# Tying TensorE's narrow products of two attention steps and of the sample rows into one visit

## The chip, the cores and the metric

The kernel runs on one core of a Trainium2 chip. The metric is the device time of one execution in microseconds (us), as the median over several runs. A profile of one further execution stands beside it. The engines are TensorE (PE, and PEld for its weight loads), VectorE (DVE), ScalarE (ACT), GpSimd (POOL) and SyncE (SP, which issues DMAs).

## The reference

One inference step of one decoder layer, in float32: 2048 prompt tokens and 8 sample tokens (one for each of 8 sequences with 2048 past tokens), model width 1024.

```python
u = x @ w_in                       # 1024 -> 7 x 512: q_a k_a v_a | q_r k_r v_r | g_r
# A: 8 heads x 64, three dilated windows (128,1), (512,4), (2048,16) with a bias on the logits;
#    the three branches are mixed in proportion to their softmax denominators
# B: 4 retention heads of 128, chunks of 128 with a decayed state, rotary q/k, per-head norm, gate
mix = concat(A, B) @ w_out
x1  = LN1(alpha * x + mix)
y   = LN2(alpha * x1 + relu(x1 @ w_up)**2 @ w_down)
```

For a sample token the attention reads 3 x 128 gathered rows of a key/value cache and its own key and value, and retention updates one 128 x 128 state for each head. Outputs are y for prompt and sample, the new key/value rows, and the retention states.

## The kernel before

Everything is kept transposed, features on the 128 partitions. The prompt is cut into four blocks j of 512 tokens. The phases follow each other: input projection of blocks 0 and 1, output projection of block 0, input projection of blocks 2 and 3, output projections of blocks 1, 2 and 3, then the feed-forward part in three passes. A float32 product with a projection or feed-forward weight is done as three products of rounded operands (high x high, high x low, low x high; `gps`, `vps` for the projections).

An input projection has 28 tiles m of 128 output features, in an order by head pair t or retention head: queries and keys of retention, the two v tiles (tiles 2 and 5, done together with x as the weights in `gemm_flip`), the gate, queries and keys of attention. Other work is woven into these tiles. Each tile calls `mid` once, which advances the attention by one step, and `end` once, which pops jobs of queues.

- **Attention steps.** `make_steps` gives a head pair in block j 4 steps (blocks 0 and 1) or 6 (blocks 2 and 3). `attn_advance` is a pipeline over them: products with v of the step before last (`attn_pv`, L687, into `o`), transposes of the last one (`attn_tr`, L656, into `ptps`), logits of a new one (`attn_qk`, L630 and L631, into `sps`). After the logits, VectorE adds the bias table and takes the row's minimum (L644), ScalarE the exponential (L645) into `p`. After the transposes, ScalarE copies those of head x = 0 (L659) and VectorE those of x = 1 (L661) to `ptile`, which has four buffers. Each product with v is 64 columns wide: the two heads of a pair write the two halves of the output's partitions. In the trace each float32 product of this kind stands as two instructions, a transpose as one.
- **Sample rows.** `sample_jobs` makes a list of jobs that `end` pops one at a time, from block 1 on: rotary, logits over gathered keys, a softmax, then for each of 8 sequences `pv(b)`: `f` (gathered values times weights, `spv`, L981) and `g` (a sum over 32-row groups, `spd`, L991, and the loads of the next sequence's values `svg`), and for each of 4 heads x 2 halves `ret(h, bh)`: `f` (state update on VectorE) and `g` (query times state, `sro`, L1026, and the loads of the next state). These products are 32 columns wide, four to a bank side by side (`tile_position`). In block 0, `v_sample` (L562, `vss`) does the sample's v rows in the same way from the raw weight tile, right where `w_split` splits that tile, twice for each t; `ev_v` then adds the four groups (`svn`, L545).
- **Retention.** `ret_stages` gives for each head and block five stages r0 to r4: transposed keys (`rtp`), scores (`rs`, L811) and state increments (`rd`, L817) with the chain of states on VectorE (`rst`, L823), outputs (`ro`, L830 and L831) and norm, transposes back (`ryt`) with the gate, store.

The code gives a program order. A scheduler with a cost model then orders the instructions of each engine: one whose operands are there, by the model, may go ahead of one traced earlier that still waits. Each engine runs its list in order. `keep_in_program_order(ins)` adds an edge for the order only, behind the instruction traced just before it on the same engine; `add_manual_dep` with class Sync adds a real dependency. `end` goes through its queues with this rule, where an entry holds a function and what it takes of two allowances t and s:

```python
t = s = 2
for q in (self.vprep, self.fin, self.rets, self.smpj):
    if q and q[0][1] <= t and q[0][2] <= s:
        f, dt, ds = q.pop(0)
        t, s = t - dt, s - ds
        f()
```

The functions that the diff touches, and their callers:

Of the kernel before, what the change touches and what calls it, by code (L numbers as in the profile page):

```python
# [9 lines left out]
F32 = mybir.dt.float32  # L10
# [50 lines left out]
class Trunk:  # L61
# [105 lines left out]
    def w_split(self, k):  # L167
        if k in self.wraw:
# [4 lines left out]
            if k in self.vsk:  # L173
                self.v_sample(*self.vsk[k], w)
# [157 lines left out]

    def gemm(self, ps, w, x, c0, n, mid=None, ks=None):
# [54 lines left out]
    def gemm_phase(self, nm, evac, mid, end, nxt=None, pre=None, before_next=None, flip=lambda m: 0):  # L388
# [3 lines left out]
        for m in range(nm - 1):  # L392
# [35 lines left out]
    def gemm_flip(self, m, evac, mid, end):  # L428
# [4 lines left out]
        for half in range(2):  # L433
            ps = self.bank(self.pg, "vps")
            for b in range(2):
                if b:
                    mid(m + half)
                    self.w_split(self.wdue)
# [9 lines left out]
    def attn_open(self):  # L448
# [13 lines left out]
        self.steps, self.sa, self.sb = [], None, None  # L462
# [76 lines left out]
    def ev_v(self, t, half, ps):  # L539
        nc, at = self.nc, self.at  # L540
        if half is None:
            v = at.tile([P, 512], F32, tag="p", name=self.nm("svn"), bufs=4)[:NB, :256]
            nc.vector.tensor_copy(v, ps[0:NB])
            for g in range(1, 4):
                nc.vector.tensor_tensor(out=v, in0=ps[32 * g:32 * g + NB], in1=v, op=OP.add)  # L545
            sl = slice(t * P, (t + 1) * P)
# [9 lines left out]
    def v_sample(self, t, half, w):  # L556

        if half == 0:
            self.vsp = self.bank(self.pt, "vss", 256)
        for k in range(4):  # L560
            g = 32 * k
            self.nc.tensor.matmul(self.vsp[g:g + NB], self.xs[:, 4 * half + k, :], w[:, 256 * k:256 * k + 256],  # L562
                                  start=(half == 0), stop=(half == 1), tile_position=(0, g))
        if half:
            self.ev_v(t, None, self.vsp)
# [28 lines left out]
    def attn_qk(self, s):  # L594
# [4 lines left out]
        for x in range(2):  # L599
# [43 lines left out]
            for d2, view, t2, dst, sl in post:  # L643
                nc.vector.tensor_tensor_reduce(d2, view, t2, 1.0, 3e38, OP.add, OP.min, sl[0])  # L644
                nc.scalar.activation(dst, dst, AF.Exp, bias=sl[0], scale=-1.0, accum_out=sl[1])  # L645
# [3 lines left out]
    def attn_tr(self, s):  # L649
        nc = self.nc  # L650
        s["PT"] = []
        tot = sum(w for _, w in s["w"])
        for x in range(2):
            b = self.bank(self.pt, "ptps", tot)
            for k in range(tot // P):
                nc.tensor.transpose(b[:, k * P:(k + 1) * P], s["P"][x][:, k * P:(k + 1) * P], self.ident)  # L656
            d = self.at.tile([P, 512], F32, tag="ptile", name=self.nm("ptile"), bufs=4)
            if x == 0:
                nc.scalar.copy(d[:, :tot], b)  # L659
            else:  # L660
                nc.vector.tensor_copy(d[:, :tot], b)  # L661
            s["PT"].append(d)

    def attn_pv(self, s):
# [6 lines left out]
        for (col, w), u in zip(s["w"], s["units"]):  # L671
            nk = w // P
            for k in range(nk):
                for x in range(2):
# [12 lines left out]
                    nc.tensor.matmul(out, v, s["PT"][x][:, col + k * P:col + (k + 1) * P],  # L687
                                     start=(k == 0), stop=(k == nk - 1))
# [1207 lines left out]
```

## Time and profile before

| what | value |
|---|---|
| median of 3 runs | 2618.89 us (2618.74 to 2621.79) |
| profiled execution, its own time | 2621.11 us |
| span of its profile, first to last instruction | 2619.3 us |
| TensorE products busy | 2571.3 us, 98% |
| TensorE weight loads busy | 2380.0 us, 91% |
| VectorE busy | 1778.6 us, 68% |
| ScalarE busy | 1260.3 us, 48% |
| mean granted TensorE clock | 0.994 |

In the profile's rows an instruction is named by its line, engine, operation, output tile and inputs (`o<-ptile,v`), then the shape (`128*64 128x128`: weights of 128 rows and 64 columns, moving operand of 128 x 128) and a count. Timeline rows give start and duration in us and merge neighbours of one kind; a matmul's duration includes its way through the array, so the time that it holds TensorE is read from start to start.

### The profile page before, as it was taken

To read this page: it belongs to the slowest core of one execution; us is meant where nothing else is said; L and a number is where in the kernel's file an instruction comes from. 1 tells how busy PE (TensorE), PEld (TensorE's weight loads), DVE (VectorE), ACT (ScalarE), POOL (GpSimd) and SP (SyncE) were. 2 spreads that over 40 slices of the span, in tenths; PEclk is the share of its full clock that TensorE was granted. 3 is DMA by queue.
4 is the path that set the end of the run, shared out by engine and by line. 5 is a ranking of instruction groups with operands and counts; after the bars stand their busy time and mean duration, and the time that the engine had idled before them with its cause. 6 is when DMAs were issued, how large, how long until landed. Compare 5 with 4: busy or idle time off the path is not lost.

```text
span 2619.3 us, 44506 instructions
## 1 busy us (share of the span) xinstructions
PE 2571.3 (98%) x16852; PEld 2380.0 (91%) x16852; DVE 1778.6 (68%) x3751; ACT 1260.3 (48%) x2632; POOL 89.2 (3%) x119
## 2 busy tenths in 40 slices
PE   8999999999999999989999999999999999999998
PEld 7999778877788788788999999999999999999998
DVE  5677886655676766679888666578775547755567
ACT  4456445444443555445565433356654336544336
POOL 0000320000110000000000000100000010000000
PEclk9999999999999999999999999999999999999999
DMA  7345764664666344578557332854484295433322
GB/s 257 115 127 181 225 184 145 210 212 141 190 193 202 117 152 148 163 228 280 204 185 261 119 113 101 306 190 153 158 265 133 93 301 197 164 111 102 100 89 76
DMA packets 233099, 451.36 MB, mean 172 GB/s; under 512 B 33665, under 2 KB 122434, under 8 KB 232339
## 3 DMA queue, kind: packets, MB, share of 16 engines
q1 hardware_dynamic: 210532, 403.07, 47.5%
q0 software_dynamic: 12864, 32.20, 3.9%
q10 hardware_dynamic: 9488, 13.24, 1.5%
q8 instruction: 133, 2.18, 0.4%
q14 instruction: 82, 0.67, 0.1%
HBM read 346.30 MB, written 102.12 MB: 171 GB/s over the span
## 4 chain that ended last, share of the span: by engine, by line
PE 51%; DMA 2%; DVE 2%; ACT 1%; issue 0%; SPq 0%; DVEq 0%; ACTq 0%
PE dps L1662 9%; PE dps L1663 9%; PE dps L1664 9%; PE ups L1603 7%; PE ups L1604 7%; PE ups L1605 7%; DMA xr<-hd 1%; PE gps L343 1%; PE gps L344 1%; PE gps L345 1%; DMA fr<-in_w_up 0%; DVE zc L1216 0%; DMA zc<-x1d 0%; DVE zc L1188 0%; DVE wl L356 0%
## 5 line engine op out<-in xcount | busy, mean ns | idle before, releaser
L1662 PE MATMUL dps<-hid,fh 128*128 128x344 f32 (+2 forms) x1544 | 487.9, 318 | 3.0 <-ACT fh L351 2.6
L1663 PE MATMUL dps<-hid,fh 128*128 128x344 f32 (+2 forms) x1544 | 490.3, 318 | 0.0
L1664 PE MATMUL dps<-hid,fl 128*128 128x344 f32 (+2 forms) x1544 | 480.0, 318 | 0.0
L1603 PE MATMUL ups<-fx,fu 128*128 128x344 f32 (+1 forms) x1344 | 429.1, 320 | 1.1 <-DVE rl L1627 0.7
L1604 PE MATMUL ups<-fx,fu 128*128 128x344 f32 (+1 forms) x1344 | 429.8, 320 | 0.0
L1605 PE MATMUL ups<-fx,fu 128*128 128x344 f32 (+1 forms) x1344 | 421.7, 319 | 0.8 <-DVE fu L356 0.6
L343 PE MATMUL gps<-xh,wh 128*128 128x512 f32 (+2 forms) x1120 | 398.7, 360 | 19.7 <-ACT xh L351 12.6
L345 PE MATMUL gps<-xh,wl 128*128 128x512 f32 (+2 forms) x1120 | 396.9, 355 | 0.9 <-DVE wl L356 0.8
L344 PE MATMUL gps<-xl,wh 128*128 128x512 f32 (+2 forms) x1120 | 397.0, 356 | 0.5 <-DVE xl L356 0.5
L351 ACT ACTIVATE fu<-fr 128x512 fp32r<-128x512 f32 x320 | 192.8, 627 | 348.1 <-PE dps L1663 235.0
L1671 DVE TENSOR_TENSOR ya<-dps,ya 128x344 f32<-128x344 f32 (+2 forms) x344 | 170.9, 504 | 194.7 <-PE dps L1664 192.8
L1662 PEld LDWEIGHTS dps<-hid,fh 128*128 128x128 f32 x1544 | 290.2, 188 | 3.5 <-ACT fh L351 2.9
L1663 PEld LDWEIGHTS dps<-hid,fh 128*128 128x128 f32 x1544 | 290.9, 188 | 0.0
L1664 PEld LDWEIGHTS dps<-hid,fl 128*128 128x128 f32 x1544 | 288.2, 188 | 0.2 <-DVE fl L356 0.2
L343 PEld LDWEIGHTS gps<-xh,wh 128*128 128x128 f32 x1120 | 212.7, 191 | 56.8 <-ACT xh L351 14.6
L1603 PEld LDWEIGHTS ups<-fx,fu 128*128 128x128 f32 x1344 | 252.6, 188 | 1.7 <-DVE rl L1627 1.0
L1604 PEld LDWEIGHTS ups<-fx,fu 128*128 128x128 f32 x1344 | 252.6, 188 | 0.0
L1605 PEld LDWEIGHTS ups<-fx,fu 128*128 128x128 f32 x1344 | 251.3, 188 | 1.3 <-DVE fu L356 1.3
L344 PEld LDWEIGHTS gps<-xl,wh 128*128 128x128 f32 x1120 | 213.7, 191 | 34.3 <-issue 5.4
L356 DVE TENSOR_TENSOR fu<-fr,fu 128x512 fp32r<-128x512 f32 x320 | 214.4, 690 | 43.0 <-ACT fu L351 41.1
L345 PEld LDWEIGHTS gps<-xh,wl 128*128 128x128 f32 x1120 | 213.7, 191 | 31.6 <-DVE wl L356 2.4
L356 DVE TENSOR_TENSOR wl<-wr,wh 128x1024 fp32r<-128x1024 f32 (+1 forms) x147 | 177.4, 1209 | 57.9 <-ACT wh L351 57.1
(256 smaller groups left out, 4269.6 us busy)
## 6 DMA issues: line engine op xcount, KB each, us to landing
wr<-in_w_in SPq DMA_DIRECT2D x111, 512.0 KB
fr<-in_w_down SPq DMA_DIRECT2D x96, 512.0 KB
fr<-in_w_up SPq DMA_DIRECT2D x64, 512.0 KB
fr<-wsd SPq DMA_DIRECT2D x64, 512.0 KB
xr<-in_x SPq DMA_DIRECT2D x64, 256.0 KB
wr<-in_w_out SPq DMA_DIRECT2D x32, 512.0 KB
wsd<-fr SPq DMA_DIRECT2D x48, 256.0 KB
t<-modd SPq DMA_DIRECT2D x16, 512.0 KB
```

Source lines behind the costliest of these rows:

```text
L343: mm(ps, wh, xh[:, c0:c0 + n], start=(k == 0), stop=False)
L344: mm(ps, wh, xl[:, c0:c0 + n], start=False, stop=False)
L345: mm(ps, wl, xh[:, c0:c0 + n], start=False, stop=(k == last))
L351: nc.scalar.activation(h, raw, AF.Copy)
L356: (nc.vector if eng_l == "v" else nc.gpsimd).tensor_tensor(out=l, in0=raw, in1=f32(h), op=OP.subtract)
L1603: mm(ps, wh, xh[:, k, :n], start=start and k == 0, stop=False, skip_group_check=not start)
L1604: mm(ps, wh, xl[:, k, :n], start=False, stop=False, skip_group_check=not start)
L1605: mm(ps, wl, xh[:, k, :n], start=False, stop=k == 3, skip_group_check=not start)
L1662: mm(ps, wh, xh, start=(k == 0), stop=False)
L1663: mm(ps, wh, xl, start=False, stop=False)
L1664: mm(ps, wl, xh, start=False, stop=(k == 3))
L1671: nc.vector.tensor_tensor(out=y, in0=ps, in1=y, op=OP.add)
```

## The change

Products with v of two attention steps, and the sample rows' 32-column products, are issued together.

- `attn_advance` keeps up to two transposed steps in `sb` and issues both steps' products with v when there are two (or when no further step is under way). Ahead of them come queued `v_sample` groups, behind them one job of the sample list that is marked "part". Such jobs (`spv`, `spd`, `sro`) are popped there alone; when nothing else is due, one goes at the second advance.
- `mm` issues a product through `pin`: within a visit, every one but the first is kept in program order behind the one before. The first product with v gets a dependency on the four copies of both steps (`cp`). The first transpose of a step gets one on the step's last exponential.
- `v_sample` is queued by `w_split` and issued at the next advance, each half in its own bank; `ev_v` adds half 0 to `svn` and then half 1. A v tile is split ahead of the `mid` call.
- In the sample list, `pm` is prepared one job ahead (`prep`), the next values are loaded in `spv`'s job, the next state in `ret`'s `f`.
- In retention's r1 the state increments and their chain come ahead of the scores, and an empty stage stands between r2 and r3.

```diff
     def w_split(self, k):
             if k in self.vsk:
-                self.v_sample(*self.vsk[k], w)
+                self.vsq.append((*self.vsk[k], w))

+    def pin(self, ins, after=()):
+        if self.visit:
+            self.tc.keep_in_program_order(ins)
+        elif self.visit == 0:
+            self.visit = 1
+        self.gate(ins, after)
+        return ins
+
+    def gate(self, ins, after):
+        for x in after:
+            self.tc.add_manual_dep(ins.ins, x.ins.name, mybir.DependencyInfo(mybir.DependencyClass.Sync,
+                                   mybir.DependencyReason.DATA), reason="visit")
+
+    def mm(self, *a, after=(), **k):
+        return self.pin(self.nc.tensor.matmul(*a, **k), after)

     # gemm_phase, ahead of mid(mm); the same in gemm_flip
+                        if k == len(w) // 2 and self.wdue in self.vsk:
+                            self.w_split(self.wdue)

     def ev_v(self, t, half, ps):
-        if half is None:
-            v = at.tile([P, 512], F32, tag="p", name=self.nm("svn"), bufs=4)[:NB, :256]
-            nc.vector.tensor_copy(v, ps[0:NB])
-            for g in range(1, 4):
+        if half in ("s0", "s1"):
+            if half == "s0":
+                self.svn = at.tile([P, 512], F32, tag="p", name=self.nm("svn"), bufs=4)[:NB, :256]
+                nc.vector.tensor_copy(self.svn, ps[0:NB])
+            v = self.svn
+            for g in range(half == "s0", 4):
                 nc.vector.tensor_tensor(out=v, in0=ps[32 * g:32 * g + NB], in1=v, op=OP.add)
+            if half == "s0":
+                return

     def v_sample(self, t, half, w):
-        if half == 0:
-            self.vsp = self.bank(self.pt, "vss", 256)
+        vsp = self.bank(self.pt, "vss", 256)
         for k in range(4):
             g = 32 * k
-            self.nc.tensor.matmul(self.vsp[g:g + NB], ..., start=(half == 0), stop=(half == 1), tile_position=(0, g))
-        if half:
-            self.ev_v(t, None, self.vsp)
+            self.mm(vsp[g:g + NB], ..., start=True, stop=True, tile_position=(0, g))
+        self.ev_v(t, "s%d" % half, vsp)

     # attn_qk keeps the step's last exponential: s["exp"] = [e]
     def attn_tr(self, s):
-                nc.tensor.transpose(b[:, k * P:(k + 1) * P], s["P"][x][:, k * P:(k + 1) * P], self.ident)
+                i = nc.tensor.transpose(b[:, k * P:(k + 1) * P], s["P"][x][:, k * P:(k + 1) * P], self.ident)
+                self.gate(i, s["exp"] if x == k == 0 else ())
...
+            s["cp"].append((nc.vector.tensor_copy if x else nc.scalar.copy)(d[:, :tot], b))

     # attn_pv(s, after)
-                    nc.tensor.matmul(out, v, s["PT"][x][:, col + k * P:col + (k + 1) * P],
-                                     start=(k == 0), stop=(k == nk - 1))
+                    self.mm(out, v, s["PT"][x][:, col + k * P:col + (k + 1) * P],
+                                     start=(k == 0), stop=(k == nk - 1), after=after)
+                    after = ()

     def attn_advance(self):
-        if self.sb is not None:
-            self.attn_pv(self.sb)
-            self.sb = None
+        part = bool(self.vsq)
+        self.visit = 0
+        for v in self.vsq:
+            self.v_sample(*v)
+        self.vsq = []
+        if len(self.sb) == 2 or (self.sb and self.sa is None):
+            part = True
+            after = [x for s in self.sb for x in s["cp"]]
+            for s in self.sb:
+                self.attn_pv(s, after)
+                after = ()
+            self.sb = []
+        if self.smpj and self.smpj[0][1] == "part":
+            self.late += 1
+            if part or self.late == 2:
+                self.smpj.pop(0)[0]()
+                self.late = 0
+        self.visit = None
         if self.sa is not None:
             self.attn_tr(self.sa)
-            self.sb, self.sa = self.sa, None
+            self.sb.append(self.sa)
+            self.sa = None

     # ret_stages: in r1 the block with "rs" and c["A"] moves behind the one with "rd" and S
-        return [(r0, 1, 0), (r1, 0, 2), (r2, 0, 1), (r3, 1, 0), (r4, 0, 0)]
+        return [(r0, 1, 0), (r1, 0, 2), (r2, 0, 1), (lambda: None, 0, 0), (r3, 1, 0), (r4, 0, 0)]

     # sample_jobs
+        def prep(b):
+            pm = c["pm"] = at.tile([P, 4, 32], F32, tag="spm", name=self.nm("spm"), bufs=2)
+            nc.gpsimd.memset(pm, 0.0)
+            nc.gpsimd.tensor_copy(pm[:, 0:3, 0:8], c["pT"][:, :, b * 8:(b + 1) * 8])
+            nc.vector.tensor_scalar(pm[0:NB, 3, 0:8], c["pn8"], self.ident[:NB, b:b + 1], None, op0=OP.mult)
     # pv(b): f uses c["pm"], issues its products by self.mm, and ends with what g ended with, and prep:
                 if b + 1 < NB:
                     for br in range(3):
                         v = ring("svg")
                         gather(b + 1, br, 1, v)
                         c["vg", b + 1, br] = v
+                    prep(b + 1)
     # ret(h, bh): ret_load of the next state moves from the end of g to the start of f; sro by self.mm
-        return [(f, 1, 0) for f in js]
+        return [(f, "part" if f in part else 1, 0) for f in js]    # part: both jobs of pv(b), g of ret

     def end(self):
-            if q and q[0][1] <= t and q[0][2] <= s:
+            if q and q[0][1] != "part" and q[0][1] <= t and q[0][2] <= s:
```

More of the change, by code (lines that the diff above doesn't have):

```diff
@@ L436, in gemm_flip @@
                 if b:
+                    if self.wdue in self.vsk:
+                        self.w_split(self.wdue)
                     mid(m + half)
@@ L461, in attn_open @@
         self.hd = [self.dram(f"hd{j}", [P, KT, TQ]) for j in range(NQ)]
-        self.steps, self.sa, self.sb = [], None, None
+        self.steps, self.sa, self.sb = [], None, []
+        self.late = 0
         self.VV, self.vdone, self.kdone, self.kdue, self.rdone = {}, set(), set(), False, set()
@@ L807, in r1 @@
         def r1():
-            b = self.bank(self.ps, "rs")
-            for i in range(4):
-                sl = slice(i * P, (i + 1) * P)
-                nc.tensor.matmul(b[:, sl], k[:, sl], q[:, sl], start=True, stop=True)
-            c["A"] = at.tile([P, 4, P], F32, tag="ra", name=self.nm("ra"))
-            nc.vector.tensor_tensor(out=c["A"], in0=b.rearrange("p (b n) -> p b n", n=P),
-                                    in1=self.mask[:, None, :].to_broadcast([P, 4, P]), op=OP.mult)
             b = self.bank(self.ps, "rd")
@@ L824, in r1 @@
                                                op0=OP.mult, op1=OP.add)
+            b = self.bank(self.ps, "rs")
+            for i in range(4):
+                sl = slice(i * P, (i + 1) * P)
+                nc.tensor.matmul(b[:, sl], k[:, sl], q[:, sl], start=True, stop=True)
+            c["A"] = at.tile([P, 4, P], F32, tag="ra", name=self.nm("ra"))
+            nc.vector.tensor_tensor(out=c["A"], in0=b.rearrange("p (b n) -> p b n", n=P),
+                                    in1=self.mask[:, None, :].to_broadcast([P, 4, P]), op=OP.mult)
         def r2():
@@ L973, in f @@
                 vs = [c.pop(("vg", b, br)) for br in range(3)] + [c["n2"]]
-                pm = at.tile([P, 4, 32], F32, tag="spm", name=self.nm("spm"), bufs=2)
-                nc.gpsimd.memset(pm, 0.0)
-                nc.gpsimd.tensor_copy(pm[:, 0:3, 0:8], c["pT"][:, :, b * 8:(b + 1) * 8])
-                nc.vector.tensor_scalar(pm[0:NB, 3, 0:8], c["pn8"], self.ident[:NB, b:b + 1], None, op0=OP.mult)
+                pm = c["pm"]
                 ps = self.bank(self.pt, "spv")
@@ L986, in f @@
                                         in1=self.sc[:, 2:10, None].to_broadcast([P, 8, 64]), op=OP.mult)
-            def g():
-                ps = self.bank(self.pt, "spd", P)
-                for t in range(4):
-                    nc.tensor.matmul(ps[32 * t:32 * t + 32, :], self.sc[:, 10:11].to_broadcast([P, 32]),
-                                     c["so"][:, t * P:(t + 1) * P], start=True, stop=True, tile_position=(0, 32 * t))
-                row(ps, self.hrow[0][b:b + 1].rearrange("b (t d) -> (b t) d", t=4))
                 if b + 1 < NB:
@@ L998, in g @@
                         c["vg", b + 1, br] = v
+                    prep(b + 1)
+            def g():
+                ps = self.bank(self.pt, "spd", P)
+                for t in range(4):
+                    self.mm(ps[32 * t:32 * t + 32, :], self.sc[:, 10:11].to_broadcast([P, 32]),
+                            c["so"][:, t * P:(t + 1) * P], start=True, stop=True, tile_position=(0, 32 * t))
+                row(ps, self.hrow[0][b:b + 1].rearrange("b (t d) -> (b t) d", t=4))
             return [f, g]
@@ L1078, in sample_jobs @@
         js += [logit(b, br) for b in range(NB) for br in range(3)]
-        js += [soft1, soft2]
+        js += [soft1, soft2, lambda: prep(0)]
+        part = []
         for b in range(NB):
             js += pv(b)
+            part += js[-2:]
         js += [ret_first]
@@ L1272, in run @@
         self.zp = xctx.enter_context(tc.tile_pool(name="zp", bufs=2, side="right"))
-        self.at, self.last_out, self.out1 = 0, False, False
+        self.at, self.last_out, self.out1, self.visit = 0, False, False, None
         self.prologue()
```

30 lines of the change are left out of this document (15 added, 15 removed).

## The prediction

> **What bounds the kernel now.** I read the page first (the span and the engines' shares), then the stages, then TensorE's timeline row by row around the products that the change moves, and last TensorE's waits in that stretch.
>
> ```profile
> span 2619.3 us, 44506 instructions
> ## 1 busy us (share of the span) xinstructions
> PE 2571.3 (98%) x16852; PEld 2380.0 (91%) x16852; DVE 1778.6 (68%) x3751; ACT 1260.3 (48%) x2632; POOL 89.2 (3%) x119
> ```
>
> The stages, one row each (columns: us, then busy time and count of PE, PEld, DVE, ACT, POOL, then granted clock, DMA share, GB/s):
>
> ```profile
> 88.00:1090.00 1002.00, 987.48 (x6755) 828.27 (x6756) 684.14 (x1663) 476.07 (x1077) 64.43 (x70) 0.99 0.55 171
> 1090.00:1180.00 90.00, 81.94 (x539) 73.43 (x537) 58.06 (x120) 33.82 (x67) 0.00 (x0) 0.96 0.62 198
> 1180.00:2619.00 1439.00, 1423.46 (x8999) 1410.01 (x8997) 981.56 (x1838) 711.49 (x1401) 22.86 (x36) 1.00 0.50 168
> ```
>
> TensorE is the limit everywhere. Attention, retention and the sample row run in the row from 88 to 1090: TensorE stands for 1002.00 - 987.48 = 14.5 us, VectorE is busy for 68%. So time taken out of TensorE's queue there should come out of the span, and the later row (feed-forward) holds nothing that the diff touches. But busy is not the same as at full rate. TensorE's timeline shows it: start, duration, operation, count of a merged run; the difference of two starts is what the run took.
>
> ```profile
> 300.03 0.40 PE L345 MATMUL gps<-xh,wl 128*128 128x512 f32 x1
> 300.36 0.43 PE L687 MATMUL o<-ptile,v 128*64 128x128 f32 x2
> 300.72 0.66 PE L656 MATMUL ptps<-ident,p 128*128 128x128 f32 x4
> 301.14 0.48 PE L343 MATMUL gps<-xh,wh 128*128 128x512 f32 x1
> 301.46 0.39 PE L344 MATMUL gps<-xl,wh 128*128 128x512 f32 x1
> 301.78 1.09 PE L687 MATMUL o<-ptile,v 128*64 128x128 f32 x14
> 302.79 0.66 PE L656 MATMUL ptps<-ident,p 128*128 128x128 f32 x4
> 303.20 0.48 PE L345 MATMUL gps<-xh,wl 128*128 128x512 f32 x1
> 303.53 0.40 PE L343 MATMUL gps<-xh,wh 128*128 128x512 f32 x1
> ```
>
> One attention step's 16 instructions with v (o, 64 columns wide) are cut here into 2 and 14. Another step is whole:
>
> ```profile
> 372.65 0.39 PE L344 MATMUL gps<-xl,wh 128*128 128x512 f32 x1
> 372.88 0.40 PE L345 MATMUL gps<-xh,wl 128*128 128x512 f32 x1
> 373.21 1.09 PE L687 MATMUL o<-ptile,v 128*64 128x128 f32 x16
> 374.24 1.09 PE L656 MATMUL ptps<-ident,p 128*128 128x128 f32 x8
> 375.08 0.48 PE L343 MATMUL gps<-xh,wh 128*128 128x512 f32 x1
> 375.40 0.39 PE L344 MATMUL gps<-xl,wh 128*128 128x512 f32 x1
> ```
>
> I call a run of 64- or 32-column products between two full-width ones a visit. Its **price beside its work**: a full-width gps product takes 372.88 - 372.65 = 0.23, but the one before the visit takes 0.33, so the way in costs 0.10. Inside, the slope comes from a shorter visit:
>
> ```profile
> 105.14 0.66 PE L687 MATMUL o<-ptile,v 128*64 128x128 f32 x8
> 105.73 0.66 PE L656 MATMUL ptps<-ident,p 128*128 128x128 f32 x4
> ```
>
> 8 instructions take 0.59, 16 take 1.03: 0.11 for two (the two heads' halves run side by side), so 8 pairs are 0.88 of the 1.03 and 0.15 is fixed. On the way out, 8 transposes and a product take 1.16 against 8 x 0.11 + 0.23 = 1.11, so 0.05 (up to 0.10 where gps follows directly). Together about 0.31 us a visit. **A split** costs more, since its first product has no partner: from 300.03 to 303.53 are 3.50 for four gps, 16 products, 8 transposes; from 372.88 to 375.40 are 2.52 for the same with two gps fewer. 3.50 - 2 x 0.23 - 2.52 = 0.52 us.
>
> Counting such runs on TensorE's timeline gives 155 visits, from the first to the last of these rows:
>
> ```profile
> 19.71 1.04 PE L562 MATMUL vss<-wr,xs 128*8 128x256 f32 x8
> ...
> 1109.62 1.09 PE L687 MATMUL o<-ptile,v 128*64 128x128 f32 x14
> ```
>
> They hold 124 runs of o and 37 of sample products (vss, spv, spd, sro), 6 of them touching. The code issues 80 steps (4 pairs of heads, 4 + 4 + 6 + 6 steps in the four blocks) and 32 sample groups of 8 instructions. So 44 steps and 5 groups stand split.
>
> **The change, part by part.**
>
> *Splits.* The first product of a visit now waits for all four copies of its two steps, and each later one is queued behind its predecessor. A first product can no longer go ahead alone: (44 + 5) x 0.52 = 25.5 us off (the sample's splits priced like the steps').
>
> *Pairing.* Two steps share one visit: 80 become 40, 40 x 0.31 = 12.4 us off.
>
> *Tying the sample groups.* I walked the queues of the changed code (one advance per tile of the projection, a tied job only where a visit is due, or alone at the second advance): 57 visits, 40 with two steps each; 15 of the 32 sample groups fall on one, 17 stand alone. What a tie saves is seen where it happened by chance:
>
> ```profile
> 788.18 0.43 PE L687 MATMUL o<-ptile,vv 128*64 128x128 f32 x2
> 788.54 0.42 PE L1026 MATMUL sro<-sst,srot 128*32 128x128 f32 x8
> 788.90 1.09 PE L687 MATMUL o<-ptile,vv 128*64 128x128 f32 x14
> ```
>
> The runs keep their 0.36 and 0.36 even side by side: between 64 and 32 columns the inner 0.15 stays, and only the way in and out, 0.10 + 0.07, goes. 15 ties less the 6 by chance: 9 x 0.17 = 1.5 us. [...]
>
> *Gates.* 80 first transposes now wait for the exponentials of both heads, and 40 first products for copies on ScalarE and VectorE. TensorE runs its list in order, so a late copy stops everything behind it, the projection's products too. What such waits cost now, in the same stretch (total, times, longest):
>
> ```profile
> PE ro L831 <- DVE rst L823: 4.6, 3, 3.2
> ...
> PE o L687 <- DVE ptile L661: 0.8, 1, 0.8
> ```
>
> 124 runs of o waited once, for 0.8. Bounds for 120 gates: nothing, or the longest wait in the list at one gate in ten, 12 x 3.2 = 38 us. I take 1.5, near the o row, since that is the same wait on the same copies. While a step waits, other products fill in, because the order is made with the wait known.
>
> *Buffers.* Four ptile buffers now hold two whole steps until their visit, so the third step's copies wait for it. They come late anyway:
>
> ```profile
> 374.98 0.58 ACT L659 COPY ptile<-ptps 128x512 f32<-128x512 f32 x1 [2.84 <-PE ptps L656]
> ...
> 375.36 0.69 DVE L661 COPY ptile<-ptps 128x512 f32<-128x512 f32 x1 [0.16 <-PE ptps L656]
> ```
>
> The first copy starts 0.74 after the first of the 8 transposes (374.24), which stand behind the visit; by then the older step's buffers are read out. I take nothing; the other end is a rival below.
>
> *Sample v rows.* The two halves go to two banks: 16 more additions on VectorE and no new product.
>
> ```profile
> L545 DVE TENSOR_TENSOR svn<-vss,svn 8x256 f32<-8x256 f32 x12 | 5.0, 420 | 0.4
> ```
>
> 16 x 0.42 = 6.7 us on VectorE, hidden under TensorE, and nobody waits for these rows for hundreds of us. If VectorE were full, at most 6.7. The raw weight tile is held until the visit, so on SP the load that takes its buffer waits, and the loads behind it: 8 times, at most a visit (1 us) each, covered by weights split two tiles ahead.
>
> *Moved loads and preparation.* 21 cache loads and 7 pairs of state loads are issued one job earlier on SP, ahead of the hrow and state stores that used to precede them; a cache load can wait there for the visit's products to free its ring slot, with weight loads behind it. POOL's memset and copy and VectorE's small product move a job ahead, count unchanged. Nothing, for the same cover. The sample's last job moves from tile 7 to tile 17 of block 3's projection by the same walk, still ahead of the last tile of the second output projection, where the queue is emptied.
>
> *Retention.* Its state chain now goes ahead of the masked scores, and an empty stage gives the normalised rows one tile more. This touches the biggest waits: 4.6 us on rst, with VectorE held up in turn and the clock down afterwards:
>
> ```profile
> 324.78 0.69 DVE L922 TENSOR_REDUCE sL<-skg 128x8 f32<-128x512 f32 x1 [2.24 <-POOL skg L921]
> ```
>
> ```profile
> 330.00:337.00 7.00, 5.93 (x28) 5.94 (x29) 6.93 (x10) 2.66 (x5) 3.81 (x3) 0.51 0.43 124
> ```
>
> At clock 0.51, these 7 us lose 3.4. Bounds: 4.6 + 3.4 = 8 us off if the lag goes, the same on top if it falls elsewhere. I take nothing, since the lag is VectorE's wait for POOL, which stays. [...]
>
> **Sum.** 25.5 + 12.4 + 1.5 - 1.5 = 37.9, say 38 us off. The profiled execution is 2621.1 us, 1.8 beyond its span; 2621.1 - 38 = 2583. The median of the runs is 2618.9, 2.2 lower: 2581 us.
>
> **Rivals.**
> *Visits fall apart again.* The pins give an order, not a neighbourhood; a full-width product may slip in wherever one in the chain is not ready. If each of the 57 breaks once, 57 x 0.31 = 17.7 come back: 2599. For it: 49 of 112 groups split now. Against: those I looked at begin with 2 of 16, the first product ahead of a partner whose copy comes later, which the gate ends.
> *The time is taken but lost again to waits*, half of it, in VectorE's lags as at 325: 2600. For it: one wait of 3.2 us also costs 3.4 of clock. Against: 14.5 us of standing in 1002.
> *Slower: the four buffers.* With two steps held, the third step's transposes fill their two PSUM banks and cannot be copied until the visit ends; retention's and the sample's transposes need the same banks, and TensorE stands. At worst a 32-instruction visit, 16 x 0.11 + 0.15 = 1.9, and a copy, 0.7, in each of 40 visits: 104 us. It decides from 38 / 40 = 0.95 a visit; at half of the worst, 1.3, it gives 52 - 38 = 14 us slower, 2633. Against: half of the buffers come free midway in the visit.
> *It does nothing*: the gates delay what they gather, and standing equals saving, 2619.
>
> **How the numbers follow.** Forecast (2567 to 2592) 0.62; visits apart or half lost (2592 to 2613) 0.22; nothing 0.07; slower 0.09. The low end takes 38, retention's 8, and 6 more for splits priced from one example off 2619; the high end takes in both half cases, 2610. Less than 0.2% (5 us) can't be told from no change here; so faster 0.84, same 0.07, slower 0.09.
>
> **What would show it.** Right: o in runs of 32 (16, 24 or 28 for the short steps), none of 2; about 57 visits; a sample run straight behind o; total standing of TensorE unchanged; rows from 1180 on the same length. Wrong: runs of o still short; new rows of waits on ptile, p or ptps with several us; a clock below 0.99 in the stretch of attention; the feed-forward part longer.

## The result, and the profile after

The changed kernel takes 2607.42 us (median of 5 runs, 2602.84 to 2608.94) against 2618.89 for the kernel before (2615.99 to 2623.03): a ratio of 0.9949 [0.9933, 0.9964], 11.5 us faster. Each kernel's own executions spread over 3 to 15 us, so differences of 5 us between two medians are not relied on below. The forecast was 2581, so the direction held and the size did not: 38 us were expected. The measured time lies above the forecast's own band (2567 to 2592) and within the wider range that ended at 2610.

The page of the changed kernel, its first lines:

```profile
span 2605.6 us, 44493 instructions
## 1 busy us (share of the span) xinstructions
PE 2545.0 (98%) x16852; PEld 2382.7 (91%) x16852; DVE 1783.7 (68%) x3767; ACT 1259.0 (48%) x2632; POOL 86.2 (3%) x119
```

The same 16852 products are busy for 26.3 us less (2571.3 - 2545.0). The visits did become whole. TensorE's timeline around one of two attention steps, and one of two steps with a sample group behind them:

```profile
382.54 0.40 PE L364 MATMUL gps<-xh,wl 128*128 128x512 f32 x1
382.87 1.97 PE L349 MATMUL o<-ptile,v 128*64 128x128 f32 x32
384.77 1.16 PE L853 MATMUL rd<-vv,kn 128*128 128x128 f32 x8
...
588.64 0.39 PE L362 MATMUL gps<-xh,wh 128*128 128x512 f32 x1
588.96 0.44 PE L349 MATMUL o<-ptile,v1prev 128*64 128x128 f32 x4
589.23 1.70 PE L349 MATMUL o<-ptile,vv 128*64 128x128 f32 x28
590.86 1.06 PE L349 MATMUL spv<-svg,spm 128*32 128x512 f32 x6
591.85 1.04 PE L349 MATMUL spv<-sn,spm 8*32 8x512 f32 x2
592.82 0.55 PE L683 MATMUL ptps<-ident,p 128*128 128x128 f32 x3
```

32 instructions take 384.77 - 382.87 = 1.90, against 2 x 1.03 and a second way in and out before. The tied visit keeps both parts' own time: 1.90 for o (590.86 - 588.96) and 1.96 for spv. A sample group that stands alone between full-width products takes the same 1.96 (from 548.16 to 550.12 in this trace). Counted on the timeline, 155 visits became 64, 124 runs of o became 43, and no run of 2 is left of 44.

Where the rest went shows in the stages, cut near the same products in each kernel (the counts differ by up to 22; columns: us, then busy time and count of PE, PEld, DVE, ACT, POOL, then granted clock, DMA share, GB/s). Before, from the attention part over the last projections to the first 300 feed-forward products:

```profile
93.98:1097.18 1003.20, 988.68 (x6740) 828.03 (x6738) 684.13 (x1660) 474.80 (x1071) 64.43 (x70) 0.99 0.55 171
1097.18:1231.50 134.32, 124.33 (x721) 106.81 (x720) 100.13 (x199) 62.62 (x120) 0.00 (x0) 0.97 0.72 233
1231.50:1279.20 47.70, 47.70 (x304) 47.70 (x303) 43.26 (x85) 31.39 (x68) 0.00 (x0) 1.00 0.76 260
```

And after:

```profile
92.40:1079.50 987.10, 959.35 (x6752) 828.28 (x6751) 685.13 (x1671) 474.89 (x1078) 61.42 (x70) 0.99 0.56 174
1079.50:1205.00 125.50, 119.18 (x707) 104.02 (x705) 90.77 (x179) 58.54 (x112) 0.00 (x0) 0.96 0.73 233
1205.00:1266.40 61.40, 57.05 (x325) 53.76 (x324) 56.14 (x110) 36.61 (x78) 0.00 (x0) 0.94 0.66 234
```

The attention part is 16.1 us shorter. TensorE is busy 29.3 us less there, but stands 987.10 - 959.35 = 27.8 against 14.5. The two rows behind it take 186.9 against 182.0: 4.9 us are lost there, with the first feed-forward products at a clock of 0.94 (their stage begins about 5 us early in the changed kernel, with the last projection products inside; so the two rows are compared together).

TensorE's longest waits after (total, times, longest):

```profile
PE gps L362 <- ACT xh L370: 9.0, 4, 5.6
PE vps L464 <- DVE rt L820: 7.6, 2, 5.5
PE ptps L683 <- DVE ptile L686: 3.7, 2, 3.2
PE rtp L847 <- ACT ptile L686: 2.8, 2, 1.8
PE gps L363 <- DVE xl L375: 2.8, 2, 2.5
```

The wait on the state row (4.6 us on rst before) is gone; waits on reads and copies out of PSUM stand in its place (rt, 3.1 before; ptile, 0.8 before and 11.0 over all rows now). And the clock: cutting the attention part where the granted clock falls gives five stretches in the changed kernel, 23.8 us at half clock together, where the kernel before had 10.2.

```profile
307.20:314.00 6.80, 5.70 (x16) 4.49 (x17) 5.25 (x9) 1.03 (x3) 2.87 (x2) 0.50 0.75 252
317.40:320.80 3.40, 3.40 (x9) 2.33 (x7) 3.39 (x8) 1.96 (x4) 0.00 (x0) 0.50 0.83 248
337.90:341.30 3.40, 3.40 (x18) 3.34 (x17) 2.34 (x11) 0.51 (x2) 1.28 (x1) 0.50 0.88 330
809.00:815.80 6.80, 5.49 (x25) 5.41 (x25) 6.70 (x22) 0.72 (x3) 1.48 (x1) 0.50 0.26 76
867.00:870.40 3.40, 3.40 (x18) 3.40 (x18) 3.37 (x12) 1.60 (x6) 0.00 (x0) 0.50 0.00 0
```

**One bookkeeping for all kernels** (but e7, which adds products of its own and has its own section). The time is the median; the other columns come from the one profiled execution of each kernel, which lies up to 5 us off its median (e13's took 2607.2, e3's 2583.2). From start to start of TensorE's instructions (a gps product lasts 0.39 us in the rows, and the next one starts 0.23 later) I take out standing (beyond 0.05 us a gap, without the start-up wait of some 6 us), then what full-width products take beyond their usual interval at half clock (0.43 in place of 0.23, as from 310.07 to 310.50 in the changed kernel), then full-rate work, the same in all kernels. What is left are the visits with their ways in and out. In the row of e8 some 10 us of the visits belong to the clock (an estimate): up to 36 us its narrower gps products take 0.21 each and right after that 0.12, the intervals of 256-column products at half clock in the changed kernel (810.69 to 810.90) and at full clock in e10 (801.78 to 801.90); but the trace of e8 has no clock for that stretch, so this is not shown.

| kernel | time, us | visits | their time | standing | lost to clock |
|---|---|---|---|---|---|
| before | 2618.9 | 155 | 161.7 | 34.3 | 11.5 |
| after | 2607.4 | 64 | 125.0 | 46.7 | 22.0 |
| e2_gate_chain | 2607.9 | 108 | 137.5 | 42.8 | 13.6 |
| e5_no_gates | 2616.7 | 121 | 150.6 | 37.8 | 14.3 |
| e1c_share | 2608.4 | 68 | 129.2 | 48.0 | 16.7 |
| e1_ptile6 | 2608.3 | 68 | 125.3 | 49.0 | 16.0 |
| e4_sample_before | 2602.9 | 75 | 130.8 | 42.1 | 15.5 |
| e8_late_reads | 2609.1 | 61 | 134.5 | 50.1 | 10.7 |
| e3_ret_before | 2587.1 | 60 | 121.0 | 35.5 | 13.0 |
| e10_no_stage | 2586.1 | 62 | 122.0 | 38.6 | 13.3 |
| e11_order | 2589.4 | 61 | 122.9 | 38.0 | 13.8 |
| e12_before_ret | 2617.6 | 150 | 158.6 | 36.7 | 12.8 |
| e13_both_before | 2602.3 | 70 | 128.1 | 44.7 | 20.0 |
| f1_stage_0to2 | 2603.6 | 64 | 123.4 | 46.0 | 19.2 |
| f2_stage_3 | 2586.2 | 62 | 122.2 | 37.3 | 13.0 |
| f3_stage_moved | 2595.4 | 63 | 123.4 | 39.8 | 17.2 |
| f4_sample_no_stage | 2608.9 | 71 | 129.4 | 50.2 | 14.3 |

For the change: 36.7 us off the visits, 12.4 more standing, 10.5 more lost to the clock; 36.7 - 12.4 - 10.5 = 13.8, and the two spans differ by 2619.3 - 2605.6 = 13.7.

### The profile page after: what moved, and what is told of

Same layout as the page of the kernel before. It is cut to its first block, busy times and chain, and to the rows that moved or that the text cites. A ratio compares the mean times of both kernels' runs of the same rounds, so it can differ in the third digit from the quotient of the medians.

```text
span 2605.6 us, 44493 instructions
## 1 busy us (share of the span) xinstructions
PE 2545.0 (98%) x16852; PEld 2382.7 (91%) x16852; DVE 1783.7 (68%) x3767; ACT 1259.0 (48%) x2632; POOL 86.2 (3%) x119
## 4 chain that ended last, share of the span: by engine, by line
PE 81%; DMA 8%; DVE 7%; ACT 1%; issue 1%; SPq 1%; POOL 0%; DVEq 0%; ACTq 0%; POOLq 0%
PE dps L1713 9%; PE dps L1714 9%; PE dps L1715 9%; PE ups L1656 8%; PE ups L1654 8%; PE ups L1655 8%; PE gps L362 5%; PE gps L363 5%; PE gps L364 5%; PE o L349 2%; PE vps L464 2%; PE vps L465 2%; PE vps L466 2%; PE ptps L683 2%; DMA ab<-ad 1%
## 5 line engine op out<-in xcount | busy, mean ns | idle before, releaser
L362 PE MATMUL gps<-xh,wh 128*128 128x512 f32 (+2 forms) x1120 | 399.1, 361 | 13.8 <-ACT xh L370 9.0
L362 PEld LDWEIGHTS gps<-xh,wh 128*128 128x128 f32 x1120 | 213.5, 192 | 47.4 <-ACT xh L370 10.5
L363 PEld LDWEIGHTS gps<-xl,wh 128*128 128x128 f32 x1120 | 215.1, 192 | 33.6 <-DVE xl L375 4.4
L671 ACT ACTIVATE p<-p,st 128x256 f32<-128x256 f32 (+3 forms) x256 | 134.2, 525 | 190.8 <-DVE st L670 188.7
```

The costliest lines, as they stand in the source:

```text
L362: mm(ps, wh, xh[:, c0:c0 + n], start=(k == 0), stop=False)
L363: mm(ps, wh, xl[:, c0:c0 + n], start=False, stop=False)
```

## The experiments

Four theories for the 23 us that came back: A, four ptile buffers are too few; B, the gates make TensorE wait; F, the drains (the prices of the visits that the change removes, 0.31 us each by the prediction's rows) were slack in which the slower lists caught up, so that waits grow with what is saved; C, each edit makes the scheduler order all lists anew, and the waits come out differently for reasons that have little to do with the edit. More came up on the way.

### Buffers: e1c_share and e1_ptile6

Two more buffers need room, so the control shares two tags first.

```diff
-            self.ge = ... tag="ge" ...;  hr = ... tag="hr" ...
+            self.ge = ... tag="rt" ...;  hr = ... tag="ra" ...          # e1c_share
-            d = ... tag="ptile", bufs=4
+            d = ... tag="ptile", bufs=6                                   # e1_ptile6, on top
```

> The changed kernel, with retention's hr in the buffer of its masked scores (ra) and the gate's temporary ge in that of rt; four ptile buffers as in the changed kernel. It is the control for the next one, which needs that room. Theories A, B and C all expect the time of the changed kernel within what another order of waits makes: 2600 to 2612.

> The control with six ptile buffers in place of four, so that a third step's copies need not wait for the visit of the two steps ahead. Theory A: TensorE's waits for banks that ptile copies hold (11 us in the changed kernel: 3.2 + 0.5 + 0.7 + 1.7 on the transposes and the projection, 1.0 + 1.8 + 1.8 on others behind ScalarE's copy) and the half clock behind them go: 10 to 18 us below the control, 2590 to 2597. Theories B and C: within 5 us of the control.

Measured: 2608.39 (ratio 0.9963 [0.9951, 0.9974]) and 2608.33 (0.9958 [0.9946, 0.9971]). Two more buffers change nothing: with six, TensorE still waits 8.3 us for VectorE's copies to ptile (9.1 in the control), 4.6 of it at the gate of o. Theory A falls.

### Gates: e2_gate_chain and e5_no_gates

The first adds to the kernel before the gates and the chain and nothing else (one step a visit); the second takes both gates out of the changed kernel.

```diff
+            self.visit = 0                                   # e2_gate_chain, in attn_advance of before
-            self.attn_pv(self.sb)
+            self.attn_pv(self.sb, self.sb["cp"])
+            self.visit = None
...
-                self.gate(i, s["exp"] if x == k == 0 else ())     # e5_no_gates
-            after = [x for s in self.sb for x in s["cp"]]
+            after = ()
```

> The kernel before, with the gates and the chain alone: each step's products with v wait for the step's own two copies and follow each other, each step's transposes wait for both exponentials; one step a visit, sample list, v_sample and retention as before. Theory A (what is lost goes to waits that holding two steps in four ptile buffers makes): no step stands split, 44 x 0.52 = 23 us off TensorE's queue, two buffers are free at any time, so waits stay near those of before (34 us standing, 27 us at half clock): 2596. Theory B (the gates themselves make TensorE stand): the same 23 off, but 15 to 25 us of new standing and half clock: 2610 to 2620. Theory C (any new order draws its waits anew, whatever is held): standing anywhere from 30 to 55 us, and none of it on ptile in particular.

> The changed kernel without its two gates: the first transpose no longer waits for both exponentials, the first product of a visit no longer for all copies. Pairs of steps, the chain and the lists stay. The changed kernel takes 2607 us, stands 52.3 us and has 54.6 us at half clock. Theory B (the gates are the waits): TensorE's standing goes back to some 42 us and the half clock to some 30, the visits stay under 75, and the time is 2585 to 2595. Theory F (the drains were slack: what TensorE saves it waits for the slower lists of VectorE and ScalarE, wherever the order puts the wait): the standing falls only as far as the visits break apart again; with some 100 visits the tile time is 10 to 12 us more, the waits 8 to 12 less, and the time is 2603 to 2611.

Measured: 2607.88 (0.9964 [0.995, 0.9977]) and 2616.73 (0.9998 [0.9985, 1.0011]). The first lies below theory B's range and 12 us above theory A's time, the second above both of its ranges. Gates and chain alone bring 155 visits to 108 and save 24.2 us of visits (44 splits and 3 visits fewer at the prediction's 0.52 and 0.31 are 24); they reach the time of the whole change. Without the gates the visits fall apart again, 121 of them, and nothing is gained: the chain alone doesn't hold a visit. Standing falls to 37.8 in e5, but kernels with the gates stand as little (37.3 to 38.6, further down), so the gates need not make TensorE wait. The lists of waits say it directly: what stops at a gate is `o` behind a copy to ptile or `ptps` behind an exponential, and the changed kernel has no such row, e10 has 1.7 us of them, e11 4.3. Theory B falls as the cause of the 23 us.

### The drains put back: e7_narrow

```diff
+            if x:                                            # between the two heads' transposes
+                nc.tensor.matmul(b[0:32, 0:P], self.ident[:, 0:32], self.ident, ..., tile_position=(0, 0))
             for k in range(tot // P):
```

> The changed kernel with one product on a 32-column tile more in each of 80 steps, between the transposes of the two heads, whose result is overwritten: it puts the drains back (80 x (0.31 + 0.05) = 29 us by the prices of the profile) while the visits stay as they are. Without theory F the time is 2607 + 29 = 2636 and the waits stay. By theory F the other lists catch up in this time: standing and half clock fall by 10 to 18 us together, and the time is 2618 to 2626.

Measured: 2629.33 (1.0039 [1.0025, 1.0054]), 22 us above the changed kernel, between the two expectations; standing 41.6 and clock loss 15.1, together 12.0 below the changed kernel. By itself this speaks for F. The kernels below have the same low values without any drains, so it settles nothing.

### VectorE's list: e8_late_reads, and the sample's list: e4_sample_before

In the changed kernel VectorE waits for DMA and for POOL in these rows, among others:

```profile
DVE nmin L764 <- DMA st<-sd: 42.0, 15, 6.0
DVE o1s L795 <- DMA ab<-ad: 35.6, 14, 6.6
DVE sst L1067 <- DMA svb<-srow: 13.4, 5, 3.7
DVE sL L965 <- POOL skg L964: 11.7, 9, 2.0
```

```diff
-            self.fin += [(fin0, 0, 0), (fin1, 1, 0), (fin2, 1, 0), (fin3, 0, 0), (fin4, 0, 0)]
+            gap = [(lambda: None, 0, 0)] * (c["j"] in (1, 2))                     # e8_late_reads
+            self.fin += [(fin0, 0, 0), *gap, (fin1, 1, 0), (fin2, 1, 0), *gap, (fin3, 0, 0), (fin4, 0, 0)]
+            # and the reduction of a sample logit runs in the next logit's job
...
-    sample_jobs of the changed kernel
+    sample_jobs of the kernel before                                              # e4_sample_before
```

> The changed kernel with VectorE's list kept from standing on others: the rows that it fetches through DRAM in the end of an attention tile (st from sd, ab from ad) are read one stage later in blocks 1 and 2, and the reduction of a sample logit one job later, when POOL has its product. In the changed kernel VectorE stands 42.0 us on st, 35.6 on ab and 11.7 on POOL's product, with copies out of PSUM behind these. Theory G (TensorE's new waits come from VectorE's list standing on DMA and POOL, with copies behind): standing of TensorE falls by 6 to 12 us, half clock by 10 to 20, and the time is 2593 to 2601. Theory F: VectorE's list has less time for the same work, and waits come at other places; 2603 to 2609.

> The changed kernel with the sample list as it was: spv, spd and sro are popped one at each end call, with their loads where they were; pairs, gates, v_sample's queue and retention's order as changed. The ties go (about 12 more visits at 0.2 to 0.3 us: 3 us on). If the sample list's moved loads and its late state loads make the wait of 5.5 us near 810 and the half clock behind it (theory D), that goes: 8 us off, about 2602 or less. Theory A: no change but the 3 us, 2610. Theory C: anywhere within 10 us.

Measured: 2609.11 (0.9963 [0.995, 0.9976]) and 2602.87 (0.995 [0.9938, 0.9962]). In e8 the waits on st and on POOL fell, the wait on ab did not, and the one on svb, which the edit does not touch, fell too:

```profile
DVE o1s L796 <- DMA ab<-ad: 37.3, 14, 6.0
DVE nmin L765 <- DMA st<-sd: 28.4, 14, 3.8
DVE sL L965 <- POOL skg L972: 9.5, 8, 1.8
DVE sst L1074 <- DMA svb<-srow: 2.0, 1, 2.0
```

That is 25.5 us less standing of VectorE in these four rows, and TensorE stood more, not less (50.1 against 46.7); theory G expected 6 to 12 us less and 2593 to 2601. Its longest waits moved: on spm and on ScalarE's ptile, which cost 0 and 1.0 us in the changed kernel, and 4.5 are left of 7.6 on rt:

```profile
PE spv L349 <- DVE spm L1025: 6.1, 1, 6.1
PE vps L464 <- DVE rt L821: 4.5, 2, 2.7
PE ptps L683 <- ACT ptile L686: 4.4, 2, 3.9
```

So taking these waits away did not bring back any of the 23 us. e4 ties fewer sample groups (75 visits) and stands a little less, with 3.7 us in place of the wait of 5.5 near 810. Its own runs lie at 2602 and at 2609, so its time can't be told from the changed kernel's; it neither shows nor excludes theory D, that the sample's later loads matter.

### Retention: e3_ret_before

```diff
         def r1():
+            (masked scores "rs", c["A"] again ahead of "rd" and the state chain)
-        return [(r0, 1, 0), (r1, 0, 2), (r2, 0, 1), (lambda: None, 0, 0), (r3, 1, 0), (r4, 0, 0)]
+        return [(r0, 1, 0), (r1, 0, 2), (r2, 0, 1), (r3, 1, 0), (r4, 0, 0)]
```

> The changed kernel with the retention's stages as before the change (masked scores ahead of the state chain, no empty stage). The prediction put this part at nothing, between 8 us off and 8 us on. If it is nothing: 2604 to 2610, with the waits on the state row back at some 5 us and others gone for it. If its order is what draws the new waits: 2594 to 2602, with standing under 46 us. If it saved what it was bounded by: 2613 to 2617.

Measured: 2587.08 (0.9883 [0.9864, 0.9901]), 20 us faster than the changed kernel, 6 from the forecast, and below all three ranges of the expectation. The visits are as whole (60) and their time is 40.7 us below before; standing and clock are back to 35.5 and 13.0. This refutes F as a law: all the drains can go without the waits growing.

### Which half of it: e10_no_stage, e11_order, e12_before_ret, e13_both_before

e10 takes out the empty stage alone, e11 restores the order of r1 alone, e12 puts both of retention's changes into the kernel before, e13 restores retention and the sample's list.

> The changed kernel without the empty stage in retention; the state chain stays ahead of the masked scores. With both parts as before the time was 2587 us, with both changed 2607. If the empty stage is the cause (the normalised rows and all that queues behind them come one tile later): 2584 to 2592, standing near 41 us. If the order of chain and scores is the cause: 2603 to 2610, standing above 48. Theory C (any other order draws its waits anew, by chance): anywhere from 2585 to 2610.

> The mirror: the changed kernel with the masked scores ahead of the state chain as before, the empty stage kept. If the empty stage is the cause: 2603 to 2610. If the order is the cause: 2584 to 2592. If each has a part: both mirrors between 2592 and 2602. Theory C: no pattern, the two mirrors and the pair need not add up.

> The kernel before with the retention's two changes alone. If they cost by themselves what they cost in the changed kernel: 2618 + 20 = 2638 (2630 to 2645), standing above 48 us. If they cost only where TensorE is ahead of the other lists: 2613 to 2623, standing 36 to 45.

> The changed kernel with retention and the sample's list both as before: gates, pairs, chain and ties stay. The one alone took 20 us off the changed kernel, the other 4.5. If they add up: 2582 (2579 to 2586). If the second only undid some of the same waits: 2585 to 2591. Theory C: 2585 to 2610.

Measured: e10 2586.08 (0.9882 [0.987, 0.9895]), e11 2589.4 (0.9893 [0.9878, 0.9907]), e12 2617.63 (1.0 [0.9991, 1.0008]), e13 2602.32 (0.9949 [0.9937, 0.996]). Undoing either half gives nearly all of the 20 us, undoing both gives no more, and both together cost nothing in the kernel before. Nor does the gain carry over: with the sample's list as before, restoring retention is worth 0.5 us (2602.87 to 2602.32). None of the halves has a price of its own: e10 alone reads as if the stage were the cause, e11 alone as if the order were. e12 also fits the rival that the two changes cost only where TensorE is ahead of the other lists; against it stand e13 beside e4, and f4 further down, where the visits are nearly as whole (70 to 75) and the same changes cost nothing.

The stages of e10, cut at the same products as above:

```profile
91.50:1061.10 969.60, 951.02 (x6751) 822.45 (x6750) 684.35 (x1672) 475.72 (x1079) 67.03 (x70) 1.00 0.56 177
1061.10:1192.20 131.10, 120.97 (x707) 104.18 (x706) 98.80 (x195) 61.62 (x118) 0.00 (x0) 0.96 0.70 231
1192.20:1245.00 52.80, 52.80 (x326) 51.79 (x325) 48.03 (x92) 35.47 (x73) 0.00 (x0) 1.00 0.74 255
```

The attention part is 33.6 us shorter than before (the changed kernel: 16.1), TensorE stands 18.6 in it, and the rows behind take 183.9. At half clock stand two stretches, 6.8 us together, instead of five with 23.8:

```profile
302.00:305.40 3.40, 3.31 (x8) 2.63 (x9) 3.37 (x3) 0.00 (x0) 2.89 (x2) 0.50 0.07 2
325.90:329.30 3.40, 3.23 (x15) 3.23 (x16) 3.32 (x6) 1.20 (x3) 1.36 (x1) 0.51 0.36 126
```

One place shows how an order makes such a wait. VectorE's timeline in the changed kernel where block 3 begins (start, duration, operation; in brackets the wait and what ended it), and TensorE's row behind it:

```profile
802.32 0.68 DVE L818 TENSOR_TENSOR rot<-gps,cs 128x512 f32<-128x512 f32 x1
802.91 0.55 DVE L686 COPY ptile<-ptps 128x384 f32<-128x384 f32 x1
806.53 1.14 DVE L1067 SCALAR_TENSOR_TENSOR sst<-svb,srot,sst 128x128 f32<-128x128 f32 x4 [3.07 <-DMA svb<-srow]
808.08 0.17 DVE L764 TENSOR_TENSOR nmin<-st 128x8 f32<-128x8 f32 x1 [0.42 <-DMA st<-sd]
808.17 0.68 DVE L818 TENSOR_TENSOR rot<-gps,cs 128x512 f32<-128x512 f32 x1
808.86 0.69 DVE L819 TENSOR_TENSOR rt<-gps,cs 64x512 f32<-64x512 f32 x1
809.57 0.68 DVE L820 TENSOR_TENSOR rt<-gps,cs 64x512 f32<-64x512 f32 x1
...
810.31 0.58 PE L464 MATMUL vps<-wh,xh 128*128 128x256 f32 x1 [5.47 <-DVE rt L820]
```

The state update of the sample (sst) and a row minimum of attention (nmin) stand ahead of the rotary reads that empty the projection's bank, and each waits for a DMA: VectorE stands 3.07 and 0.42, TensorE 5.47, and the clock is halved from 809.0 for 6.8 us. As nmin could not start before 808.08, moving sst alone would not have freed the reads earlier. In e10 the same instructions stand the other way round (nmin follows at 803.73):

```profile
800.00 0.69 DVE L819 TENSOR_TENSOR rt<-gps,cs 64x512 f32<-64x512 f32 x1
800.71 0.68 DVE L820 TENSOR_TENSOR rt<-gps,cs 64x512 f32<-64x512 f32 x1
...
802.69 0.60 DVE L1067 SCALAR_TENSOR_TENSOR sst<-svb,srot,sst 128x128 f32<-128x128 f32 x2
...
801.44 0.39 PE L464 MATMUL vps<-wh,xh 128*128 128x256 f32 x1 [1.86 <-DVE rt L820]
```

1.86 of standing instead of 5.47, and the clock stays. With half of the 5.49 us that TensorE is busy there at half clock, this place makes some 3.6 + 2.7 = 6.3 of the 17.5 us between the two attention parts (an estimate); the rest is not traced. The edit that makes the difference is an empty stage in retention, a job that holds no instruction at all.

### Where the empty stage stands: f1_stage_0to2, f2_stage_3, f3_stage_moved, f4_sample_no_stage

```diff
-... (r2, 0, 1), (lambda: None, 0, 0), (r3, 1, 0), (r4, 0, 0)]
+... (r2, 0, 1), *[(lambda: None, 0, 0)] * (j < NQ - 1), (r3, 1, 0), (r4, 0, 0)]     # f1
+... (r2, 0, 1), *[(lambda: None, 0, 0)] * (j == NQ - 1), (r3, 1, 0), (r4, 0, 0)]    # f2
+... (r2, 0, 1), (r3, 1, 0), (lambda: None, 0, 0), (r4, 0, 0)]                       # f3
+... (r2, 0, 1), (r3, 1, 0), (r4, 0, 0)]                    # f4, on e4_sample_before
```

> The changed kernel with the empty stage of retention in blocks 0 to 2 only, not in block 3, whose end opens the feed-forward part. Everywhere 2607, nowhere 2586. Theory E (the end of attention comes too late for the first rows' layer norm): the first 300 feed-forward products take 48 us and not 61.5 - 5.2 = 56, and the time is 2596 to 2600. Theory C (each order draws its waits): between 2583 and 2610, without regard to that row.

> The mirror: the empty stage in block 3 only. Theory E: the feed-forward part's first 300 products take 55 to 57 us, the attention part is that of the kernel without the stage (2586), and the time is 2593 to 2597. Theory C: between 2583 and 2610, and the first 300 products may as well take 48.

> The changed kernel with the empty stage behind the normalised rows (ahead of their store) and not ahead of them: as many stages, the same walk through the lists. If the length of retention's list costs (theory E): 2603 to 2610, first 300 products 55 to 57 us. If the lateness of the normalised rows costs: 2584 to 2590. Theory C: anywhere from 2583 to 2610.

> The changed kernel with the sample's list as before (2602.9 with the empty stage) and without the empty stage. If the stage costs by itself what it costs in the changed kernel: 2603 - 20 = 2583 (2580 to 2590). Theory C: no fixed amount; 2585 to 2610, and the kernel with the sample's list and the whole of retention as before, at 2602, speaks for that.

Measured: f1 2603.57 (0.9942 [0.9929, 0.9954]), f2 2586.23 (0.9879 [0.9861, 0.9897]), f3 2595.35 (0.9911 [0.9898, 0.9925]), f4 2608.94 (0.9963 [0.9949, 0.9977]). Theory E (attention ends too late for the first feed-forward rows) falls: with the stage in block 3 alone the first 300 feed-forward products take 47.8 us, not 55 to 57, and without it there 50.7. Its late start of the feed-forward part is real in the changed kernel (4.9 us of the stages above), but it follows the order, not the length of the list (f3 and e11 have the stage in block 3 too, and take 47.8 and 47.9). With the same number of stages f3 lies between. f4's median is 6 us above e4's, and their runs overlap: the stage that costs 20 us in one kernel costs nothing in another.

after, e3, e10, e11, f1, f2 and f3 hold the same work, differ only in the order in which it is written, and spread over 21 us (2586.1 to 2607.4); their visits take 121.0 to 125.0. The spread that theory C speaks of is thus shown for these seven; its forecasts were so wide (2583 to 2610) that hitting them says little. The place above can be followed through all seven traces. In the changed kernel and f1 both sst and nmin stand ahead of the reads, and TensorE waits 5.47 and 5.63; in e10, e3, f2 and f3 both stand behind, and it waits 1.86 in each; in e11 sst stands ahead but comes earlier, and it waits 2.38. So the order of the lists carries this wait, and the two slowest kernels are the two that have it. For the rest of the spread that is not shown. Open is also whether a rule lies behind the good orders: the stage costs in blocks 0 to 2 (f1) and not in block 3 (f2), but only with the new order of r1 (e11) and the new sample list (f4).

e10, e3 and f2 beat both kernels: 2586 to 2587, 0.988 of the time before.

## Why the prediction was right in direction and wrong in size

- **Splits, pairing, ties** (25.5 + 12.4 + 1.5 = 39.4 expected): right. The visits' time fell by 36.7 in the changed kernel, 38.3 to 40.7 in the kernels with the same work. 64 visits stand instead of 57: the 15 ties are there, and 3 steps and 4 sample groups are still split.
- **No extra loss at a tie.** 1.90 and 1.96 side by side (from 588.96 over 590.86 to 592.82) are the two runs' own times; the row shows no loss beyond the 0.15 inside each run, as the prediction took it.
- **Gates** (1.5): not refuted. Waits at a gate are nothing in the changed kernel, 1.7 us in e10, 4.3 in e11. What the prediction missed is what they are for: without them the visits fall apart (e5).
- **Buffers** (nothing): right (e1_ptile6).
- **Sample rows, moved loads** (nothing): not separable. With the sample's list as before the time is the same within the noise in one kernel (e4), 15 and 23 more in two others (e13 against e3, f4 against e10).
- **Standing and clock: this is the step that failed.** The sum lets 1.5 us of new waits in, at the gates, and takes TensorE's other standing (14.5 us in the attention part) and its clock as they were. Measured are 12.4 us more standing and 10.5 more lost to the clock, 22.9 against 1.5, and hardly any of it at the gates. The prediction had asked of each edit which wait it moves, on the order of before; an order is made of all edits together, and the longest new wait came on rt (5.5 us), which no part of the change touches.
- **Retention** (nothing, at most 8 either way) is the term where this shows most. In this kernel undoing it gives 18 to 21 us. Its work was not mis-sized: in the kernel before it is worth nothing (e12). So 20 us is not its price, but what the order that came with it cost here.
- **The rival "taken, but lost again to waits, half of it"** is what happened, with more than half lost: 2600 forecast, 2607 measured. Its cause is borne out in part: over all rows TensorE waits 6.8 us longer for VectorE and 4.3 longer for ScalarE. The clock's share is about as large as it said: 10.5 of 22.9.
- **What would show it:** the runs of o and the ties came as written; total standing did not. Of its signs of being wrong two came true: waits behind ptile copies (11.0 us), and 4.9 us more for the last projections with the first feed-forward products.

## What to carry to other kernels

Where one edit makes a scheduler order everything anew, as here, the time of one version holds an order's luck: estimate the work saved from the rows, and put an order's worth of waits (here some 20 us of 2600) into the range. Before a part is judged, take it out alone and shift something that costs nothing, such as an empty stage; if that moves the time as much as the part does, pick the best of several orders. On an engine that runs its list in order, look for instructions that wait for a DMA and stand ahead of copies out of PSUM (here VectorE stood 3.07 us on svb ahead of the rotary reads, and TensorE 5.47 behind them).

## What the runs showed of the hardware

- **Half clock came behind standing.** In the traces of before and after, from 40 us on and without the last 15 us, the granted clock falls to half 14 times, 9 times for 3.4 us and 5 times for 6.8. In the 3.4 us just before these falls TensorE stands 1.57 to 3.41 us. In the attention part these are 2.25 and 1.86 before 330.1 and 354.0 in the kernel before, and 2.07, 2.54, 1.74, 3.41 and 1.97 before 307.2, 317.4, 337.9, 809.0 and 867.0 in the changed kernel. In the first 3.4 us of the five long stretches TensorE stands 0.97 to 1.36 us, in the nine short ones at most 0.54. The length of a wait alone does not tell: in the changed kernel the wait of 1.74 us before 336.5 was followed by half clock, the one of 1.98 us before 355.1 was not. The prediction had set 3.4 us of clock beside the whole wait of 3.2 us before 331.07 in the kernel before; the clock fell at 330.1, inside that wait, after 2.25 us of it. A wait with half clock behind it thus cost more than its own length: up to 1.7 us for each 3.4 us at half clock (an estimate, half of 3.4).
- **A chain alone does not keep products together.** This is the scheduler's doing. In e5 each product is ordered behind the one before it, and there are still 121 visits; with the gates as well there are 64.
